# Four of eighteen key tiles transposed on TensorE instead of by DMA, in a two-branch attention layer

## The chip, the cores and the metric

The kernel runs on one core of one Trainium2 chip. The metric is the device time of one execution in microseconds (us); of several runs of the same kernel the median counts. [...]

## What is computed

One layer over 2048 latent tokens of width 1024, with 256 context tokens in front of the keys, so that each query sees 2304 keys. Two kinds of attention read the same projection: eight heads of latent attention (the first kind, `kind` 0: query and key of 96 columns, values of 64) and four heads of differential attention (the second kind, `kind` 1: two score maps of 64 columns each, values of 128). Both outputs pass gates and projections, are merged, projected again and normalised.

```python
def _softmax_attend(q, k, v, scale):
    s = jnp.einsum('bhqd,bhkd->bhqk', q, k).astype(jnp.float32) * scale
    p = jax.nn.softmax(s, axis=-1).astype(v.dtype)
    return jnp.einsum('bhqk,bhkd->bhqd', p, v)

def _diff_attend(q1, q2, k1, k2, v, lam, scale):
    s1 = jnp.einsum('bhqd,bhkd->bhqk', q1, k1).astype(jnp.float32) * scale
    s2 = jnp.einsum('bhqd,bhkd->bhqk', q2, k2).astype(jnp.float32) * scale
    p = jax.nn.softmax(s1, axis=-1) - lam * jax.nn.softmax(s2, axis=-1)
    return jnp.einsum('bhqk,bhkd->bhqd', p.astype(v.dtype), v)
...
    o_a = _blockwise(lambda q: _softmax_attend(q, k_mla, v_mla, MLA_SCALE), (q_mla,))
    o_d = _blockwise(lambda q1, q2: _diff_attend(q1, q2, k1, k2, dv, lam, DIFF_SCALE),
                     (dq[:, :, 0], dq[:, :, 1]))
```

## The kernel before

The kernel has three stages. The first (to about 930 us) projects the tokens and writes queries, keys, values and gates to DRAM. The second (about 935 to 2630 us) is the attention; the gate projections that the first stage left over fill its TensorE order as `gate_units` (tiles `fhT`, `fw`, `pf`, `fo`). The third merges, projects and normalises. Numbers are carried as a high part and a low part, so a product is two or three matmuls.

The attention runs over units of one head and 256 queries: 64 units of the first kind and 32 of the second, interleaved two to one (`units`, lines 810 to 814). A unit has two tiles of 128 queries. For such a tile `softmax_tile` computes the scores against the 2304 keys in three stretches of 768 columns, each in a PSUM tile `ps` of 1024 columns (pool `cps`, three buffers): per operand pair one matmul of 512 columns and one of 256 (line 669), three pairs for the first kind, two for each map of the second. VectorE empties `ps` into `s` and carries the running minimum along (line 670); ScalarE then makes the exponential of all 2304 columns in place (line 683) with the row sum. There are 256 such score tiles, 128 of each kind; in the second kind two maps are combined on VectorE (line 773) before they go on, which leaves 64.

`transposed` (line 689) then brings the 192 probability tiles into the layout that the product with the values needs, keys on the partitions. It takes a tile in two halves of 1152 columns, that is nine key tiles of 128: ScalarE casts the half to float16 (`hl`, line 693), GpSimd subtracts that from `s` for the low part (line 694; VectorE does one of two in the last units), and a DMA transpose on the SP queue (line 695) moves both parts as 18 blocks of 128x128 into `pts`. `hl` has four buffers, `pts` two units' worth, `s` five. Four units later in the written order the products with the values read `pts` through `pt_part` (lines 710, 723, 728).

`load_v` (line 790) makes the float16 parts of a head's values at the head's first unit, chunk by chunk of 384 columns: ScalarE scales and casts (line 804), VectorE scales again and subtracts (line 805). There are 48 chunks: three for each of eight heads, six for each of four.

The written order gives priorities; the final order on each engine is laid out ahead of the run by a planner that works with its own estimates of times. At run time each engine takes its instructions in that fixed order.

Of the kernel before, what the change touches and what calls it, by code (L numbers as in the profile page):

```python
# [9 lines left out]
F32 = mybir.dt.float32  # L10
F32R = mybir.dt.float32r
F16 = mybir.dt.float16
I32 = mybir.dt.int32
AF = mybir.ActivationFunctionType
ALU = mybir.AluOpType
PSUM = bass.MemoryType.PSUM
DRAM = bass.MemoryType.DRAM

P = 128
# [31 lines left out]
LEAD = 1  # L51
SPN = 3
LAG = 4

O_CQ, O_CKV, O_KR, O_GA, O_DQ, O_DK, O_DV, O_GD, O_MG = (
    0, 384, 640, 672, 1184, 1696, 2208, 2720, 3232)
# [5 lines left out]
def layer_kernel(ctx: ExitStack, tc: tile.TileContext, x, c, ctxt, c_ctx, w_mod, b_mod, w_in,  # L62
# [3 lines left out]
    pe, dve, act, pool, sp = nc.tensor, nc.vector, nc.scalar, nc.gpsimd, nc.sync  # L66
# [92 lines left out]
    with ExitStack() as st:  # L159
# [133 lines left out]
        for t in range(2):  # L293
            c0 = O_CKV + t * P
# [282 lines left out]

    with ExitStack() as st:
        kp, qp_, vp = {}, {}, {}
        kp[1] = st.enter_context(tc.tile_pool(name="ck1", bufs=3))  # L580
        qp_[1] = st.enter_context(tc.tile_pool(name="cq1", bufs=1))
        vr = st.enter_context(tc.tile_pool(name="cvr", bufs=2))
        vp[1] = st.enter_context(tc.tile_pool(name="cv1", bufs=1))
        kp[0] = st.enter_context(tc.tile_pool(name="ck0", bufs=3))
        qp_[0] = st.enter_context(tc.tile_pool(name="cq0", bufs=2))
        spool = st.enter_context(tc.tile_pool(name="cs", bufs=5))
        sm = st.enter_context(tc.tile_pool(name="csm", bufs=12))
# [5 lines left out]
        fr = st.enter_context(tc.tile_pool(name="fr", bufs=FB, side="right"))  # L593
        fw = st.enter_context(tc.tile_pool(name="fw", bufs=FB, side="right"))
        fo = st.enter_context(tc.tile_pool(name="fo", bufs=1, side="right"))
        ps_s = st.enter_context(tc.tile_pool(name="cps", bufs=3, space=PSUM))
        ps_f = st.enter_context(tc.tile_pool(name="cpf", bufs=1, space=PSUM))
        ps_o = st.enter_context(tc.tile_pool(name="cpo", bufs=1, space=PSUM))

# [61 lines left out]
        def softmax_tile(qk, ks, scale, shift, zsum):  # L661
            s = spool.tile([P, NT], F32, tag="s", name="s")
            z = sm.tile([P, 4], F32, tag="z", name="z")
            for g in range(3):
                ps = ps_s.tile([P, 1024], F32, tag="ps", name="ps")
                for i, (qa, sel) in enumerate(qk):
                    ka = sel(ks[g])
                    for c0, n in ((0, 512), (512, 256)):
                        pe.matmul(ps[:, c0:c0 + n], qa, ka[:, c0:c0 + n], start=(i == 0), stop=(i == len(qk) - 1))  # L669
                dve.tensor_scalar(s[:, g * 768:(g + 1) * 768], ps[:, :768], -scale, 3e38 if g == 0 else z[:, g - 1:g],  # L670
                                  op0=ALU.mult, op1=ALU.min, accum_out=z[:, g:g + 1])

            b = z[:, 2:3]
            if isinstance(shift, float):
                dve.tensor_scalar(z[:, 0:1], z[:, 2:3], z[:, 2:3], 2.0 ** 40, op0=ALU.mult, op1=ALU.is_lt)
                dve.tensor_scalar(z[:, 1:2], z[:, 0:1], shift, z[:, 2:3], op0=ALU.mult, op1=ALU.add)  # L676
                b = z[:, 1:2]
            elif shift is not None:
                dve.tensor_scalar(z[:, 0:1], z[:, 2:3], -1.0, z[:, 2:3], op0=ALU.mult, op1=ALU.min)
                dve.tensor_scalar(z[:, 0:1], z[:, 0:1], 2.0 ** -22, shift, op0=ALU.mult, op1=ALU.add)  # L680
                dve.tensor_scalar(z[:, 1:2], z[:, 0:1], z[:, 2:3], None, op0=ALU.add)
                b = z[:, 1:2]
            mark[0] = act.activation(s, s, AF.Exp, bias=b, scale=-1.0, accum_out=zsum).ins  # L683
            return s

        def new_pts():
            return [ptp.tile([P, 2, 9, 2, P], F16, tag="pt", name="pt") for _ in range(2)]

        def transposed(pts, i, s, shared):
            for e in range(2):  # L690
                hl = p16.tile([P, 2, 1152], F16, tag="hl", name="hl")
                se = s[:, e * 1152:(e + 1) * 1152]
                act.copy(hl[:, 0], se)  # L693
                (dve if shared and e else pool).tensor_tensor(hl[:, 1], se, hl[:, 0], op=ALU.subtract)  # L694
                sp.dma_start_transpose(pts[e][:, :, :, i, :].rearrange("p l k q -> p (l k) q"),
                                       hl.rearrange("p l n -> p (l n)"))

        def pt_part(pts, kt, l):
            return pts[kt // 9][:, l, kt % 9].rearrange("p i q -> p (i q)")

        def av_end(po, dst):
            o = op_.tile([P, 256], F32, tag="o", name="o")
# [46 lines left out]
        def mla_soft(h, u, qt, ks, pts):  # L749
            for i in range(2):  # L750
                qs = qt[0:96, :, i * P:(i + 1) * P]
                k_hi, k_lo = (lambda k: k[0:96, 0, :]), (lambda k: k[0:96, 1, :])
                s = softmax_tile([(qs[:, 0, :], k_hi), (qs[:, 0, :], k_lo), (qs[:, 1, :], k_hi)], ks, MLA_SCALE, LN_PSC,
                                 zs[u][:, i, h:h + 1])
                transposed(pts, i, s, n_ >= len(units) - 2)
                yield

        def diff_soft(h, u, qt, ks, pts):
            for i in range(2):
                def scores(m, shift, zsum):  # L760
                    qs = qt[:, m, :, i * P:(i + 1) * P]
                    km = (lambda k: k[:, m, :])
                    return softmax_tile([(qs[:, 0, :], km), (qs[:, 1, :], km)], ks, DIFF_SCALE, shift, zsum)


                za = zs[u][:, i, H + h:H + h + 1]
                sa = scores(0, lamc[:, 2:3], za)
                yield
                w = sm.tile([P, 3], F32, tag="w", name="w")
                sb = scores(1, None, w[:, 0:1])  # L770
                dve.reciprocal(w[:, 1:2], w[:, 0:1])
                dve.tensor_scalar(w[:, 2:3], za, w[:, 1:2], lamc[:, 0:1], op0=ALU.mult, op1=ALU.mult)
                dve.scalar_tensor_tensor(sa, sb, w[:, 2:3], sa, op0=ALU.mult, op1=ALU.add)  # L773
                transposed(pts, i, sa, n_ >= len(units) - 3)
                yield

        def load_k(kind, h):
            ks = []
            for g in range(3):
                k = kp[kind].tile([P, 2, 768], F32R, tag=f"k{kind}", name=f"k{kind}")  # L780
                cs = slice(g * 768, (g + 1) * 768)
                if kind == 0:
                    ldma(k[0:64], kn_s[h // 2][(h % 2) * 64:(h % 2) * 64 + 64, :, cs])
                    ldma(k[64:96], kr_s[:, :, cs])
                else:
                    ldma(k, dk_s[h][:, :, :, cs].rearrange("l d m n -> (l d) m n"))
                ks.append(k)
            return ks

        def load_v(kind, h):  # L790
# [10 lines left out]
            for t in range(0, NKT, nt):  # L801
                raw = vr.tile([P, nt, 64 * (1 + kind)], F32, tag="vr", name="vraw")
                ldma(raw, src[:, t:t + nt, :])
                act.activation(hi[:, t:t + nt, :], raw, AF.Identity, scale=sv)
                dve.scalar_tensor_tensor(lo[:, t:t + nt, :], raw, sv, hi[:, t:t + nt, :], op0=ALU.mult, op1=ALU.subtract)
            return vt


# [252 lines left out]
```

## Time and profile before

| | us |
|---|---|
| median of three runs | 3048.63 |
| lowest and highest run | 3046.4, 3067.55 |
| the profiled execution | 3054.12 |
| its span, first to last instruction | 3052.3 |
| TensorE busy | 2753.9 |
| VectorE busy | 1787.6 |
| GpSimd busy | 1581.8 |
| ScalarE busy | 1446.9 |

The profile is of one execution. A slice is a fortieth of the span, about 76 us. Idle time of an engine is put down to what ended it; matmuls overlap, so that the busy time of TensorE is not a measure of how fully it is used. PE is TensorE's matmuls, PEld its weight loads, DVE VectorE, ACT ScalarE, POOL GpSimd, SP the queue that issues most of the DMAs; a q behind an engine's name is its sequencer.

### The profile page before, as it was taken

Reading aid. Unit: us, or ns where it says so; the run is one execution under the profiler, and the core shown is the slowest. Engines: PE = TensorE matmul, PEld = TensorE weight load, DVE = VectorE, ACT = ScalarE, POOL = GpSimd, SP = SyncE. Lnnn points to the kernel's source line nnn. Section 1 sums busy time; section 2 is a strip of 40 time slices with the busy share of each in tenths; the row PEclk is TensorE's granted clock in tenths of the full one; section 3 lists DMA queues with packets and bytes.
Section 4 is the critical chain, followed back from the end, with each engine's and each line's share of the span. In section 5 each row is a group of like instructions: output and inputs, shape, how many; then the busy total and the mean of one; then the engine's idle time right before and its main releaser. Section 6 shows DMA issues by size and latency. Waiting matters only on the chain.

```text
span 3052.3 us, 44693 instructions
## 1 busy us (share of the span) xinstructions
PE 2753.9 (90%) x16177; PEld 2241.3 (73%) x16177; DVE 1787.6 (59%) x3583; ACT 1446.9 (47%) x1757; POOL 1581.8 (52%) x922
## 2 busy tenths in 40 slices
PE   7999999999998988979888899889889787789998
PEld 5888888879777766757666677667667665789886
DVE  4476310024766757767666577666676688575444
ACT  3333222233335656756666576656577566321110
POOL 2442222232444666857666567657567566363344
PEclk9999999999999999989999899989899898899999
DMA  8567533364487999999999999999999998977542
GB/s 253 128 184 226 158 90 97 94 217 140 133 245 193 206 195 200 194 220 214 188 207 198 236 226 205 204 189 182 222 209 205 196 209 164 241 210 210 181 137 89
DMA packets 1273377, 571.93 MB, mean 187 GB/s; under 512 B 950250, under 2 KB 1222336, under 8 KB 1273156
## 3 DMA queue, kind: packets, MB, share of 16 engines
q1 hardware_dynamic: 1149448, 463.59, 70.5%
q10 hardware_dynamic: 123708, 105.49, 15.0%
q8 instruction: 127, 2.08, 0.3%
q14 instruction: 94, 0.77, 0.1%
HBM read 224.16 MB, written 118.30 MB: 112 GB/s over the span
## 4 chain that ended last, share of the span: by engine, by line
DMA 20%; PE 18%; issue 6%; ACT 6%; DVE 6%; POOL 5%; ACTq 1%; SPq 1%; POOLq 0%; DVEq 0%
DMA pt<-hl 16%; PE pz L995 6%; PE ps L669 5%; POOL hl L694 4%; ACT s L683 3%; ACT hl L693 2%; DVE s L670 2%; PE po L723 1%; PE po L710 1%; DMA mg<-gt 1%; POOL fw L108 1%; PE po L728 1%; DMA fraw<-in_w_in_dram 1%; DMA g<-gt 1%; PE py L114 1%
## 5 line engine op out<-in xcount | busy, mean ns | idle before, releaser
L694 POOL TENSOR_TENSOR hl<-s,hl 128x1152 f16<-128x1152 f32 x378 | 939.9, 2502 | 470.7 <-ACT hl L693 432.7
L669 PE MATMUL ps<-k,q 96*128 96x256 f32 (+3 forms) x3840 | 840.1, 359 | 54.4 <-DVE s L670 47.2
L669 PEld LDWEIGHTS ps<-k,q 96*128 96x128 f32 (+1 forms) x3840 | 624.0, 197 | 176.3 <-DVE s L670 58.3
L670 DVE TENSOR_SCALAR_CACHE_REDUCE s<-ps,z 128x768 f32<-128x768 f32 x512 | 518.4, 1014 | 207.5 <-PE ps L669 197.7
L693 ACT CAST hl<-s 128x1152 f16<-128x1152 f32 x384 | 433.3, 1148 | 430.1 <-DMA pt<-hl 259.8
L683 ACT ACTIVATE s<-s,z 128x2304 f32<-128x2304 f32 x256 | 566.9, 2215 | 71.9 <-DVE z L676 34.2
L112 PE MATMUL pp<-hT,w 128*128 128x512 f32 (+1 forms) x896 | 350.3, 393 | 4.8 <-DVE qa L331 2.5
L108 POOL TENSOR_TENSOR w<-raw,w 128x512 fp32r<-128x512 f32 (+1 forms) x126 | 164.5, 1311 | 362.8 <-ACT w L105 346.3
L113 PE MATMUL pp<-hT,w 128*128 128x512 f32 (+1 forms) x896 | 351.8, 393 | 0.0
L114 PE MATMUL pp<-hT,w 128*128 128x512 f32 (+1 forms) x896 | 350.3, 392 | 0.0
L670 DVE TENSOR_SCALAR_CACHE_REDUCE s<-ps 128x768 f32<-128x768 f32 x256 | 243.9, 953 | 77.5 <-PE ps L669 66.7
L710 PE MATMUL po<-pt,vd 128*128 128x256 f16 x1728 | 237.3, 282 | 27.2 <-DMA pt<-hl 27.2
L723 PE MATMUL po<-pt,va 128*128 128x256 f16 x1152 | 177.3, 296 | 88.2 <-DMA pt<-hl 88.1
L710 PEld LDWEIGHTS <-vd 128*128 128x128 f16 x1728 | 157.9, 101 | 81.2 <-issue 50.5
L723 PEld LDWEIGHTS <-va 128*128 128x128 f16 x1152 | 107.3, 105 | 142.9 <-issue 91.5
L108 POOL TENSOR_TENSOR fw<-fraw,fw 128x512 fp32r<-128x512 f32 x84 | 143.3, 1706 | 120.2 <-ACT fw L105 114.4
L112 PEld LDWEIGHTS pp<-hT,w 128*128 128x128 f32 x896 | 170.1, 190 | 44.3 <-DVE qa L331 3.0
L114 PEld LDWEIGHTS pp<-hT,w 128*128 128x128 f32 x896 | 170.3, 190 | 38.2
L113 PEld LDWEIGHTS pp<-hT,w 128*128 128x128 f32 x896 | 170.3, 190 | 37.7 <-POOL hT L266 0.4
L773 DVE SCALAR_TENSOR_TENSOR s<-s,w 128x2304 f32<-128x2304 f32 x64 | 195.7, 3058 | 0.5
L995 PE MATMUL pz<-wz,yt 128*128 128x512 f32 x768 | 179.6, 396 | 0.8 <-DVE z L998 0.8
L995 PEld LDWEIGHTS pz<-wz,yt 128*128 128x128 f32 x768 | 144.3, 188 | 35.8 <-DVE z L998 1.3
(222 smaller groups left out, 4384.1 us busy)
## 6 DMA issues: line engine op xcount, KB each, us to landing
raw<-in_w_in_dram SPq DMA_DIRECT2D x122, 256.0 KB, 3.1
fraw<-in_w_in_dram ACTq DMA_DIRECT2D x79, 256.0 KB, 4.7
xt<-in_x_dram SPq DMA_DIRECT2D x32, 512.0 KB, 5.1
mg<-gt SPq DMA_DIRECT2D x64, 256.0 KB, 3.8
q<-dq ACTq DMA_DIRECT2D x60, 256.0 KB, 6.3
gt<-o SPq DMA_DIRECT2D x54, 256.0 KB, 2.0
gt<-fo ACTq DMA_DIRECT2D x42, 256.0 KB, 4.2
kn<-kst SPq DMA_DIRECT2D x36, 256.0 KB, 3.3
```

The costliest lines, as they stand in the source:

```text
L108: eng_lo.tensor_tensor(lo, t32, hi.bitcast(F32) if hi.dtype == F32R else hi, op=ALU.subtract)
L112: pe.matmul(ps, wh, mh, start=first, stop=False)
L113: pe.matmul(ps, wh, ml, start=False, stop=False)
L114: pe.matmul(ps, wl, mh, start=False, stop=last)
L669: pe.matmul(ps[:, c0:c0 + n], qa, ka[:, c0:c0 + n], start=(i == 0), stop=(i == len(qk) - 1))
L670: dve.tensor_scalar(s[:, g * 768:(g + 1) * 768], ps[:, :768], -scale, 3e38 if g == 0 else z[:, g - 1:g], op0=ALU.mult, op1=ALU.min, accum_ ...
L683: mark[0] = act.activation(s, s, AF.Exp, bias=b, scale=-1.0, accum_out=zsum).ins
L693: act.copy(hl[:, 0], se)
L694: (dve if shared and e else pool).tensor_tensor(hl[:, 1], se, hl[:, 0], op=ALU.subtract)
L710: pe.matmul(po, vv[:, w, kt, :], pt_part(pts, kt, l), start=(kt == 0 and i == 0), stop=(kt == NKT - 1 and i == 2))
L723: pe.matmul(po, vv[:, kt, :], pt_part(pts, kt, 0), start=(kt == 0), stop=(kt == NKT - 1))
L995: pe.matmul(pz[:, n, :], y[:, yy, k, :], wz[k][ww][:, n * 512:(n + 1) * 512], start=(k == 0 and i == 0), stop=(k == KT - 1 and i == 2))
```

## The change

In the first kind, four of the eighteen key tiles of each probability tile (tiles 5 to 8, the end of the first half) no longer go through the cast, the subtraction and the DMA transpose. TensorE transposes them in float32 into a PSUM tile `px` of 512 columns, ScalarE copies this as the high part into `pts`, and VectorE subtracts for the low part. The first DMA transpose of such a tile then has 10 blocks instead of 18; the second kind and the second half stay at 18. In `hl` and `pts` the high and low block of a key tile now lie side by side.

The scores are computed in stretches of 1024, 768 and 512 columns, each with a PSUM pool and a key tile of its own size. Per operand pair that is five matmuls instead of six. The space for `px` comes from this.

In `load_v`, GpSimd scales the loaded values in place, ScalarE casts them, and GpSimd subtracts.

```diff
+NCB = 5
+GS = ((0, 1024), (1024, 768), (1792, 512))
...
-        ps_s = st.enter_context(tc.tile_pool(name="cps", bufs=3, space=PSUM))
+        ps_s = [st.enter_context(tc.tile_pool(name=f"cps{g}", bufs=1, space=PSUM)) for g in range(3)]
+        ps_x = st.enter_context(tc.tile_pool(name="cpx", bufs=1, space=PSUM))
...
-            for g in range(3):
-                ps = ps_s.tile([P, 1024], F32, tag="ps", name="ps")
+            for g, (k0, nk) in enumerate(GS):
+                ps = ps_s[g].tile([P, nk], F32, tag="ps", name="ps")
                 for i, (qa, sel) in enumerate(qk):
                     ka = sel(ks[g])
-                    for c0, n in ((0, 512), (512, 256)):
-                        pe.matmul(ps[:, c0:c0 + n], qa, ka[:, c0:c0 + n], start=(i == 0), stop=(i == len(qk) - 1))
-                dve.tensor_scalar(s[:, g * 768:(g + 1) * 768], ps[:, :768], -scale, 3e38 if g == 0 else z[:, g - 1:g],
+                    for c0 in range(0, nk, 512):
+                        c1 = min(c0 + 512, nk)
+                        pe.matmul(ps[:, c0:c1], qa, ka[:, c0:c1], start=(i == 0), stop=(i == len(qk) - 1))
+                dve.tensor_scalar(s[:, k0:k0 + nk], ps, -scale, 3e38 if g == 0 else z[:, g - 1:g],
                                   op0=ALU.mult, op1=ALU.min, accum_out=z[:, g:g + 1])
...
-            return [ptp.tile([P, 2, 9, 2, P], F16, tag="pt", name="pt") for _ in range(2)]
+            return [ptp.tile([P, 9, 2, 2, P], F16, tag="pt", name="pt") for _ in range(2)]
-        def transposed(pts, i, s, shared):
-            for e in range(2):
-                hl = p16.tile([P, 2, 1152], F16, tag="hl", name="hl")
-                se = s[:, e * 1152:(e + 1) * 1152]
-                act.copy(hl[:, 0], se)
-                (dve if shared and e else pool).tensor_tensor(hl[:, 1], se, hl[:, 0], op=ALU.subtract)
-                sp.dma_start_transpose(pts[e][:, :, :, i, :].rearrange("p l k q -> p (l k) q"),
-                                       hl.rearrange("p l n -> p (l n)"))
+        def transposed(pts, i, s, shared, ncb):
+            for e, n in enumerate((ncb, 9)):
+                hl = p16.tile([P, 9, 2, P], F16, tag="hl", name="hl")[:, :n]
+                se = s[:, e * 1152:e * 1152 + n * P].rearrange("p (k q) -> p k q", q=P)
+                act.copy(hl[:, :, 0], se)
+                (dve if shared and e else pool).tensor_tensor(hl[:, :, 1], se, hl[:, :, 0], op=ALU.subtract)
+                sp.dma_start_transpose(pts[e][:, :n, :, i, :].rearrange("p k l q -> p (k l) q"),
+                                       hl.rearrange("p k l q -> p (k l q)"))
+            for k0 in range(ncb, 9, 4):
+                px = ps_x.tile([P, 4, P], F32, tag="px", name="px")
+                for t in range(4):
+                    pe.transpose(px[:, t, :], s[:, (k0 + t) * P:(k0 + t + 1) * P], ident)
+                hi, lo = (pts[0][:, k0:k0 + 4, l, i, :] for l in range(2))
+                act.copy(hi, px)
+                dve.tensor_tensor(lo, px, hi, op=ALU.subtract)
...
-                transposed(pts, i, s, n_ >= len(units) - 2)
+                transposed(pts, i, s, n_ >= len(units) - 2, NCB)
...
-                transposed(pts, i, sa, n_ >= len(units) - 3)
+                transposed(pts, i, sa, n_ >= len(units) - 3, 9)
...
-            for g in range(3):
-                k = kp[kind].tile([P, 2, 768], F32R, tag=f"k{kind}", name=f"k{kind}")
-                cs = slice(g * 768, (g + 1) * 768)
+            for g, (k0, nk) in enumerate(GS):
+                k = kp[kind].tile([P, 2, nk], F32R, tag=f"k{kind}{g}", name=f"k{kind}{g}")
+                cs = slice(k0, k0 + nk)
...
-                act.activation(hi[:, t:t + nt, :], raw, AF.Identity, scale=sv)
-                dve.scalar_tensor_tensor(lo[:, t:t + nt, :], raw, sv, hi[:, t:t + nt, :], op0=ALU.mult, op1=ALU.subtract)
+                pool.tensor_scalar(raw, raw, sv, None, op0=ALU.mult)
+                act.copy(hi[:, t:t + nt, :], raw)
+                pool.tensor_tensor(lo[:, t:t + nt, :], raw, hi[:, t:t + nt, :], op=ALU.subtract)
```

## Rows read from the trace of the kernel before

**Rows 1.** The page: engine busy us (share) xinstructions, then tenths in 40 slices.

```profile
PE 2753.9 (90%) x16177; PEld 2241.3 (73%) x16177; DVE 1787.6 (59%) x3583; ACT 1446.9 (47%) x1757; POOL 1581.8 (52%) x922
...
PEclk9999999999999999989999899989899898899999
DMA  8567533364487999999999999999999998977542
```

**Rows 2.** Stretches view, inner attention: us, busy by engine, clock, DMA share, GB/s.

```profile
1000.00:2500.00 1500.00, 1316.19 (x8035) 1024.98 (x8033) 1025.26 (x2099) 980.17 (x968) 979.85 (x423) 0.92 1.12 205
```

**Rows 3.** DMA view, 1000 to 2500 us: packets, MB, share; issues, median us to landing.

```profile
q1 hardware_dynamic: 806782, 206.83, 82.3%
q10 hardware_dynamic: 115168, 99.78, 29.0%
...
pt<-hl SPq DMA_TRANSPOSE x345, 6.8
```

**Rows 4.** Line 695 (ns min/median/max, first and last start), and SP's timeline from 1500 us.

```profile
L695 SPq DMA_TRANSPOSE pt<-hl x384: 2169/3342/14507, 961.4 to 2621.3; - x192
...
1497.88 142.65 SPq L695 DMA_TRANSPOSE pt<-hl  x34
```

**Rows 5.** The chain of work, 1000 to 2500 us: shares by line.

```profile
by line: DMA pt<-hl 32.0%; issue 10.7%; PE ps L669 9.6%; POOL hl L694 6.8%; ACT s L683 6.3%; ACT hl L693 3.9%; PE po L723 2.7%; DVE s L670 2.5%; POOL fw L108 2.1%; PE po L710 1.9%; PE po L728 1.9%; DMA fraw<-in_w_in_dram 1.8%; DVE s L773 1.
```

**Rows 6.** Waits from 950 to 2600 us: us in total, times, longest us.

```profile
PE po L723 <- DMA pt<-hl: 85.2, 25, 10.6
PE ps L669 <- DVE s L670: 47.2, 35, 4.7
PE po L710 <- DMA pt<-hl: 27.2, 17, 4.9
...
ACT hl L693 <- DMA pt<-hl: 258.0, 124, 12.8
```

**Rows 7.** TensorE's timeline, first stage: start us, us, engine, line, operation.

```profile
644.52 0.39 PE L112 MATMUL pp<-hT,w 128*128 128x512 f32 x1
644.75 1.03 PE L261 MATMUL pt<-ident,xt 128*128 128x128 f32 x8
645.54 0.48 PE L113 MATMUL pp<-hT,w 128*128 128x512 f32 x1
```

**Rows 8.** TensorE's timeline in the attention.

```profile
1321.92 4.39 PE L669 MATMUL ps<-k,q 96*128 96x512 f32 x24
1326.15 0.40 PE L114 MATMUL pf<-fhT,fw 128*128 128x512 f32 x1
1326.39 0.39 PE L112 MATMUL pf<-fhT,fw 128*128 128x512 f32 x1
```

**Rows 9.** Groups by line: shape xcount | busy us, mean ns | idle before, releasers.

```profile
L694 POOL TENSOR_TENSOR hl<-s,hl 128x1152 f16<-128x1152 f32 x378 | 939.9, 2502 | 470.7 <-ACT hl L693 432.7 <-DVE s L670 7.0 <-DVE z L680 6.6
...
L693 ACT CAST hl<-s 128x1152 f16<-128x1152 f32 x384 | 433.3, 1148 | 430.1 <-DMA pt<-hl 259.8 <-DVE s L773 68.0 <-PE ps L669 20.4
...
L805 DVE SCALAR_TENSOR_TENSOR va<-vraw,vsc,va 128x384 f16<-128x384 f32 x24 | 37.5, 1575 | 29.0 <-ACT va L804 29.0
...
L805 DVE SCALAR_TENSOR_TENSOR vd<-vraw,vsc,vd 128x384 f16<-128x384 f32 x24 | 29.7, 1254 | 9.9 <-ACT vd L804 9.9
```

**Rows 10.** Single lines: engine, operation, ns min/median/max, first and last start us.

```profile
L641 ACT ACTIVATE fo<-pf x42: 571/587/600, 955.1 to 2403.0; 128x512 f32<-128x512 f32 x42
...
L643 DVE SCALAR_TENSOR_TENSOR fo<-fo,pf x16: 671/682/689, 956.2 to 1941.0; 128x512 f32<-128x512 f32 x16
...
L926 POOL TENSOR_TENSOR uf<-ab x32: 720/742/1247, 2503.8 to 2824.2; 128x256 f32<-128x256 f32 x32
...
L872 POOL TENSOR_TENSOR rawe<-rawe,gb x16: 1270/1364/1891, 2661.7 to 2731.4; 128x512 f32<-128x512 f32 x16
```

**Rows 11.** Stretches of 50 us, columns as in rows 2.

```profile
1300.00:1350.00 50.00, 36.80 (x221) 28.71 (x220) 26.80 (x60) 26.55 (x26) 22.62 (x11) 0.86 1.17 225
...
1800.00:1850.00 50.00, 47.27 (x312) 36.40 (x311) 41.67 (x82) 36.74 (x38) 33.32 (x14) 1.00 1.17 220
```

More of the change, by code (lines that the diff above doesn't have):

```diff
@@ L579, in layer_kernel @@
         kp, qp_, vp = {}, {}, {}
-        kp[1] = st.enter_context(tc.tile_pool(name="ck1", bufs=3))
+        kp[1] = st.enter_context(tc.tile_pool(name="ck1", bufs=1))
         qp_[1] = st.enter_context(tc.tile_pool(name="cq1", bufs=1))
@@ L583, in layer_kernel @@
         vp[1] = st.enter_context(tc.tile_pool(name="cv1", bufs=1))
-        kp[0] = st.enter_context(tc.tile_pool(name="ck0", bufs=3))
+        kp[0] = st.enter_context(tc.tile_pool(name="ck0", bufs=1))
         qp_[0] = st.enter_context(tc.tile_pool(name="cq0", bufs=2))
@@ L686, in new_pts @@
         def new_pts():
-            return [ptp.tile([P, 2, 9, 2, P], F16, tag="pt", name="pt") for _ in range(2)]
-        def transposed(pts, i, s, shared):
-            for e in range(2):
-                hl = p16.tile([P, 2, 1152], F16, tag="hl", name="hl")
-                se = s[:, e * 1152:(e + 1) * 1152]
-                act.copy(hl[:, 0], se)
-                (dve if shared and e else pool).tensor_tensor(hl[:, 1], se, hl[:, 0], op=ALU.subtract)
-                sp.dma_start_transpose(pts[e][:, :, :, i, :].rearrange("p l k q -> p (l k) q"),
-                                       hl.rearrange("p l n -> p (l n)"))
+            return [ptp.tile([P, 9, 2, 2, P], F16, tag="pt", name="pt") for _ in range(2)]
[14 more added lines that the diff above has]
+                dve.tensor_tensor(lo, px, hi, op=ALU.subtract)
         def pt_part(pts, kt, l):
-            return pts[kt // 9][:, l, kt % 9].rearrange("p i q -> p (i q)")
+            return pts[kt // 9][:, kt % 9, l].rearrange("p i q -> p (i q)")
         def av_end(po, dst):
```

## The prediction

> **What bounds the kernel now.** I read the page first: TensorE is busy 90% of the span, and the slices show that the DMA engines run at 9 tenths or more through the middle half, just where TensorE's granted clock is no longer steady [rows 1]. That half is the attention stage, so everything below is read from it, mostly from its inner 1500 us. There TensorE is busy 1316 us, ScalarE 980, GpSimd 980, VectorE 1025, and the DMA share is 1.12, that is, packets of two queues overlap on the same engines all the time; the mean granted clock is 0.92 [rows 2]. [...]
>
> So no compute engine but TensorE is near its limit, and TensorE still idles 184 us. The DMA view of the same stretch says what fills the engines: 82.3% is the SP queue, 29.0% the ScalarE queue [rows 3]; in this stretch the SP queue is almost only the transposes of the split probabilities, 345 of them. The SP rows give the pace: 384 transposes between 961 and 2624 us, 4.3 us each, of which the issuing instruction alone holds the queue 3.34 us at the median, 2.17 at best, 14.5 at worst; the timeline shows 34 of them in one unbroken piece of 142.65 us, 4.2 us each [rows 4]. They run one behind another with little between them. The chain inside the stretch agrees: the landing of a transpose (`pt<-hl`) is 32.0% of it, four times any other single line but `issue` [rows 5]. The waits show how it reaches the engines: ScalarE stands 258 us in 124 waits because a `hl` buffer is not back from its transpose; GpSimd's idle time before the subtraction ends mostly with ScalarE's cast, 433 of 471 us [rows 9]; TensorE waits 85 and 27 us for `pt` and 47 us for VectorE to empty a score buffer [rows 6].
>
> The stage is thus paced by a loop, cast, subtract, transpose, buffer back, with TensorE close behind as the second limit.
>
> **The change part by part.** *Fewer transposed blocks.* A transpose moves 18 blocks of 128 columns (9 high, 9 low). For the first kind (128 score tiles of the 192 that are transposed) the first of two moves only 10. That is 128 of 384 transposes cut by 8/18, 14.8% of all blocks. The trace has no transpose of 10 blocks, so its price lies between no saving and the proportional one: 4.3 us x 8/18 x 128 = 245 us of queue time at the pace of [rows 4], 123 us at the best case of 2.17 us. The DMA share speaks for proportional: the engines are full of these packets, and their number falls with the blocks. What reaches the end is the part on the chain: 32.0% of the 1663 us stage is 532 us, and 14.8% of that is **79 us** saved. [...]
>
> *Shorter casts and subtractions.* The 1152-column subtraction on GpSimd takes 2.50 us, the cast on ScalarE 1.15 [rows 9]. With 640 columns I take the subtraction as proportional, -1.1 us x 128 = -136 us of GpSimd work. For ScalarE I use the line between 0.587 us at 512 columns (`fo`, [rows 10]) and 1.148 at 1152, about 0.70 at 640: -0.45 x 128 = -57 us of work. On the chain these lines are 6.8% and 3.9% [rows 5], 113 and 65 us of the stage; 15% of the first and 13% of the second are **17 and 8 us** saved. That the new layout of `hl` (high and low of a block side by side) is written in pieces of 128 costs nothing by any row here; if it slows GpSimd by a tenth, that is some 90 us of its work with 9% of the chain, 8 us.
>
> *The four blocks on TensorE.* 512 transposes of 128x128 in f32. The nearest rows are the transposes of x in the first stage: eight of them between two matmuls start at 644.75 and the next matmul at 645.54, 0.10 us each [rows 7]. That is 51 us of TensorE. [...] I take half: **+26 us**. They are emptied by ScalarE (128 x 0.587 = 75 us) and VectorE (128 x 0.682 = 87 us, the 512-column operation that reads PSUM) [rows 10]. ScalarE thus ends at +18 us, VectorE at +20 after losing the value split below. The ScalarE lines are 10.2% of the chain, so its added 75 us is taken at **+8 us**, VectorE's at +1.
>
> *New waits.* Before, TensorE never waited for the exponential; with five `s` buffers it could run several tiles ahead. Now its in-order queue has, once per tile of the first kind, a transpose that needs the exponential, and the next scores, the values' products and the gate projections stand behind it. ScalarE in turn waits for TensorE before it copies `px`, with the next exponential behind that copy. Bounds: nothing, if the order leaves room, and 128 x 2.1 us (the mean of ScalarE's 124 waits) = 269 us. The nearest wait of the same sort, TensorE for VectorE at a score buffer, is 47 us over 768 stretches; I take **+10 us**.
>
> *Stretches of 1024, 768, 512.* Columns are the same; one of six matmuls per operand pair goes. 24 score matmuls, 12 pairs of 512+256, take 4.23 us up to the next matmul's start, 0.352 a pair, and a lone 512-column matmul 0.24 to the next [rows 8], so the 256-column one costs about 0.12: half of a 512-column one, and two small ones cost what a large one does. No gain beyond the last eviction before the exponential, 512 instead of 768 columns; the first is longer by as much. Zero; with the buffers still three, a loss needs TensorE to wait for the 1024-column one, and the 47 us could grow by a third, 16 us.
>
> *Values on GpSimd.* 48 chunks of 384 columns lose a VectorE operation (37.5 and 29.7 us in all, [rows 9]) and gain two on GpSimd, a scaling and a subtraction. GpSimd takes 0.742 us for 256 columns and 1.364 for 512 [rows 10], so about 1.05 for 384: +101 us of work, in bursts of 6 us for a head of the first kind and 13 for the second, ahead of `hl` subtractions, which wait. At GpSimd's 9% of the chain it is **+9 us**; bounds 0 and 101.
>
> *The clock.* In [rows 11], 50 us stretches with 36.8 us of TensorE work have a granted clock of 0.86, those with 47.3 have 1.00: less waiting for `pt` gives clock back. [...]
>
> **Sum.** -79 -17 -8 +26 +8 +1 +10 +9 -10 = -60 us. The profiled execution took 3054.1 us (span 3052.3), so 2994 for its like; it lies 5.5 us above the median of the runs, so the forecast is **2989 us**, 2.0% faster. Its own range is 2950 to 3015.
>
> **The rivals.**
>
> *The queue frees the whole stage.* If transposes alone pace it, the queue's own saving counts, 123 to 245 us, less TensorE's 51. Speaking for it: the unbroken SP pieces and a DMA share over 1. Against: TensorE is busy 88% of the stretch and takes over soon. A saving of 110 to 170 us, about 2905.
>
> *TensorE is the bound, or the burden only moves.* The saved landing time is latency that the two units of buffered `pt` hide anyway, and TensorE's 51 us, GpSimd's 101 us burst and the new waits eat the rest. It also covers a short transpose that costs nearly what a long one does. Then the sum is -25 to +30 us, about 3045; with all 101 us of the value split on the path and the forecast's other terms it is +32, about 3080, the end of this case. [...]
>
> *Slower: TensorE stands at the transposes.* ScalarE is late by 2.1 us at 124 places now, and every one of these delays the exponential behind it; TensorE did not feel it, and now does. Price: with 1.2 us a tile on average, 128 x 1.2 = 154 us instead of my 10, the sum is +84 us, about 3130. It decides from 0.6 us a tile (77 us) on, where the sum is above zero. For it speaks that both in-order queues now wait for each other; against, that exponential and transpose can be placed some microseconds apart with other matmuls between them.
>
> **How the numbers follow.** Chances: forecast 0.44, whole stage freed 0.17, burden moves 0.23, TensorE stands 0.16. About 1% (30 us) is what a measurement of this kernel can tell from no change. Faster by over 1% takes the first two, 0.61; within 1% 0.23; slower 0.16. The range goes from 2900, the end of the second case, to 3070, the upper part of the third; it leaves out most of the fourth and a little of the second, some 0.2.
>
> **What would show it.** Right: the SP queue's transposes keep to 384 but a third of them at 10/18 of the time; DMA share in the stage near 1.0; ScalarE's wait for `pt<-hl` well under 258 us; the granted clock above 0.92. `px` waits of TensorE (on `s` from line 683's exponential) under 20 us in all. Wrong: that wait at 80 us or more (TensorE stands), a short transpose at 3 us (no saving), or GpSimd's `hl` late behind the value split.

## The result

| | before | after |
|---|---|---|
| median of the runs, us | 3047.52 (4 runs, 3034.46 to 3067.55) | 2967.98 (4 runs, 2960.77 to 2979.64) |
| the profiled execution, us | 3054.12 | 2964.99 |

The ratio is 0.9716, with a 95% interval from 0.9674 to 0.9758: 2.8% faster, where 2.0% was forecast (2989 us, range 2900 to 3070). In the two profiled executions the difference is 89 us where the sum said 60.

The page of the kernel after (engine busy us and share; in 40 slices the clock that TensorE was granted, in tenths of its full one, and DMA), to be held against [rows 1]:

```profile
PE 2761.3 (93%) x16049; PEld 2210.5 (75%) x16049; DVE 1777.4 (60%) x3663; ACT 1446.5 (49%) x1885; POOL 1522.9 (51%) x1018
...
PEclk9999999999999999999999999999999998899999
DMA  8467533364568999999999999999999998877542
```

TensorE does about the same busy time in a shorter span, and the slices of its clock that fell to 8 in the attention stage are gone until the very end of the stage. The inner 1500 us (columns as in [rows 2]) and the DMA view of the same stretch (as in [rows 3]):

```profile
1000.00:2500.00 1500.00, 1384.61 (x8279) 1044.20 (x8279) 1091.28 (x2309) 1026.16 (x1136) 956.20 (x520) 0.96 1.04 193
```

```profile
q1 hardware_dynamic: 727232, 187.35, 75.1%
q10 hardware_dynamic: 116446, 100.94, 28.7%
...
pt<-hl SPq DMA_TRANSPOSE x362, 5.7
```

TensorE's idle time in these 1500 us went from 184 to 115 us, its clock from 0.92 to 0.96, the DMA share from 1.12 to 1.04, and 362 transposes fit where 345 did, with a tenth fewer packets. The waits from 950 to 2600 us, as in [rows 6]:

```profile
PE po L737 <- DMA pt<-hl: 34.2, 9, 6.6
PE ps L674 <- DVE s L675: 21.2, 20, 3.4
PE po L724 <- DMA pt<-hl: 20.9, 15, 4.8
PE px L707 <- DVE pt L710: 20.0, 8, 8.7
...
PE px L707 <- ACT s L688: 2.3, 2, 1.9
...
ACT hl L700 <- DMA pt<-hl: 197.2, 82, 10.8
...
ACT pt L709 <- PE px L707: 19.7, 12, 4.4
```

TensorE's two waits for `pt` fell from 112 to 55 us, its wait for score buffers from 47 to 21. The new wait on the exponential is 2.3 us in all; the new wait that does show is 20.0 us for the one `px` tile to be emptied.

The single prices stand in the groups by line and shape (columns as in [rows 9]):

```profile
L701 POOL TENSOR_TENSOR hl<-s,hl 128x640 f16<-128x640 f32 x128 | 181.2, 1415 | 100.0 <-ACT hl L700 94.2 <-DVE z L686 2.8 <-DVE pt L710 1.0
...
L700 ACT CAST hl<-s 128x640 f16<-128x640 f32 x128 | 92.3, 721 | 79.2 <-DMA pt<-hl 65.6 <-DMA k<-kn 8.0 <-POOL hl L701 2.3
L710 DVE TENSOR_TENSOR pt<-px,pt 128x512 f16<-128x512 f32 x128 | 87.8, 686 | 147.4 <-ACT pt L709 146.9 <-DMA q<-qn 0.3
L707 PE MATMUL px<-ident,s 128*128 128x128 f32 x512 | 81.9, 285 | 22.4 <-DVE pt L710 20.0 <-ACT s L688 2.3
...
L709 ACT CAST pt<-px 128x512 f16<-128x512 f32 x128 | 73.5, 574 | 28.1 <-PE px L707 19.7 <-issue 4.6 <-POOL fw L110 1.8
```

All of them are near what was put down: 1.42 us for the short subtraction (1.39 by proportion), 0.72 for the short cast (0.70), 0.574 and 0.686 for emptying `px` (0.587 and 0.682).

### The profile page after: what moved, and what is told of

Read it like the earlier page. It is cut to its first block, busy times and chain, and to the rows that moved or that the text cites. A ratio compares the mean times of both kernels' runs of the same rounds, so it can differ in the third digit from the quotient of the medians.

```text
span 2963.2 us, 44826 instructions
## 1 busy us (share of the span) xinstructions
PE 2761.3 (93%) x16049; PEld 2210.5 (75%) x16049; DVE 1777.4 (60%) x3663; ACT 1446.5 (49%) x1885; POOL 1522.9 (51%) x1018
## 5 line engine op out<-in xcount | busy, mean ns | idle before, releaser
L701 POOL TENSOR_TENSOR hl<-s,hl 128x1152 f16<-128x1152 f32 (+1 forms) x378 | 784.6, 2092 | 440.6 <-ACT hl L700 408.7
L674 PE MATMUL ps<-k,q 96*128 96x512 f32 (+3 forms) x3200 | 822.3, 391 | 25.0 <-DVE s L675 21.8
L674 PEld LDWEIGHTS ps<-k,q 96*128 96x128 f32 (+1 forms) x3200 | 546.1, 193 | 145.2 <-DVE s L675 38.4
L700 ACT CAST hl<-s 128x1152 f16<-128x1152 f32 (+1 forms) x384 | 375.5, 1007 | 362.0 <-DMA pt<-hl 197.2
L675 DVE TENSOR_SCALAR_CACHE_REDUCE s<-ps,z 128x768 f32<-128x768 f32 (+1 forms) x512 | 450.4, 880 | 104.8 <-PE ps L674 84.3
L675 DVE TENSOR_SCALAR_CACHE_REDUCE s<-ps 128x1024 f32<-128x1024 f32 x256 | 312.1, 1219 | 129.7 <-PE ps L674 106.2
L787 DVE SCALAR_TENSOR_TENSOR s<-s,w 128x2304 f32<-128x2304 f32 x64 | 183.5, 2867 | 0.1
L710 DVE TENSOR_TENSOR pt<-px,pt 128x512 f16<-128x512 f32 x128 | 87.8, 686 | 147.4 <-ACT pt L709 146.9
```

Source lines behind the costliest of these rows:

```text
L674: pe.matmul(ps[:, c0:c1], qa, ka[:, c0:c1], start=(i == 0), stop=(i == len(qk) - 1))
L675: dve.tensor_scalar(s[:, k0:k0 + nk], ps, -scale, 3e38 if g == 0 else z[:, g - 1:g], op0=ALU.mult, op1=ALU.min, accum_out=z[:, g:g + 1])
L700: act.copy(hl[:, :, 0], se)
L701: (dve if shared and e else pool).tensor_tensor(hl[:, :, 1], se, hl[:, :, 0], op=ALU.subtract)
```

## The experiments

Each ratio is to the kernel before, measured beside it on the same chip (its median there 3053 to 3060 us). Moving one part lets the planner lay out a new order for every engine. In the traces, ScalarE, VectorE and GpSimd run the attention stage of e9 in exactly the changed kernel's order, instruction by instruction; in e2, e5, e10 and e12 they do not, and neither do e1, e3 and e4 keep the order of the kernel before. So each of these runs tests its part together with a new order.

| run | median us | ratio, 95% interval |
|---|---|---|
| e1: no blocks on TensorE | 3091.94 | 1.0096 (1.0061 to 1.0131) |
| e2: values back on VectorE | 2973.28 | 0.9730 (0.9684 to 0.9777) |
| e3: stretches alone | 3069.26 | 1.0046 (1.0021 to 1.0071) |
| e4: value split alone | 3055.98 | 0.9986 (0.9959 to 1.0013) |
| e5: all blocks moved anyway | 3061.74 | 1.0008 (0.9967 to 1.0050) |
| e6: TensorE's blocks as an extra | 3094.84 | 1.0145 (1.0099 to 1.0190) |
| e7: eight blocks | 3085.91 | 1.0122 (1.0080 to 1.0163) |
| e8: both kinds | 2977.03 | 0.9763 (0.9724 to 0.9802) |
| e9: old layout | 2966.44 | 0.9695 (0.9652 to 0.9738) |
| e10: a buffer of its own | 3050.72 | 0.9984 (0.9954 to 1.0014) |
| e11: eight blocks, `px` in halves | 3591.41 | 1.1761 (1.1699 to 1.1824) |
| e12: five shared buffers | 2972.97 | 0.9731 (0.9692 to 0.9770) |

The theory was that fewer transposed blocks make the gain and that TensorE is the next limit. The rivals were that the stretches, the relief of VectorE, or the shorter casts and subtractions make it.

### Which part carries the gain: e1 to e4

e1 is the changed kernel with all 18 key tiles on the DMA:

```diff
-NCB = 5
+NCB = 9
...
-        ps_x = st.enter_context(tc.tile_pool(name="cpx", bufs=1, space=PSUM))
+        ps_x = None
```

> The changed kernel with all 18 key tiles back on the DMA transpose; the stretches, the layout of hl and pt and the values on GpSimd stay. If fewer transposed blocks are the cause (theory), nearly the whole gain of 80 us goes: 3030 to 3065 us, with 384 transposes at 4.2 us or more apart and a DMA share of 1.1 in the stage. If the stretches, the layout or the value split carry the gain (rivals), it stays under 3000 us.

It took 3092 us, 1.0% slower than the kernel before and above the expected range. Not only the gain goes, what is left of the change costs something. Its inner stage and its transposes (ns min/median/max):

```profile
1000.00:2500.00 1500.00, 1287.86 (x7302) 960.14 (x7300) 960.83 (x2020) 957.07 (x950) 1031.70 (x494) 0.92 1.11 201
```

```profile
L702 SPq DMA_TRANSPOSE pt<-hl x384: 2380/3322/14449, 946.4 to 2629.8; - x192
```

Clock, DMA share and transposes are those of [rows 2, 4].

e2 takes the changed kernel and puts `load_v` back as it was:

```diff
-                pool.tensor_scalar(raw, raw, sv, None, op0=ALU.mult)
-                act.copy(hi[:, t:t + nt, :], raw)
-                pool.tensor_tensor(lo[:, t:t + nt, :], raw, hi[:, t:t + nt, :], op=ALU.subtract)
+                act.activation(hi[:, t:t + nt, :], raw, AF.Identity, scale=sv)
+                dve.scalar_tensor_tensor(lo[:, t:t + nt, :], raw, sv, hi[:, t:t + nt, :], op0=ALU.mult, op1=ALU.subtract)
```

> The changed kernel with the value split back on VectorE. Theory: worth little either way, 2950 to 2985 us; the sum of the prediction had it at +9 us, so about 2960 without it. If the relief of VectorE carries the gain (rival), 3000 us or more.

2973 us: no difference to the changed kernel that the intervals show.

e3 is the kernel before with the stretches of 1024, 768 and 512 columns and the key tiles that go with them:

```diff
+GS = ((0, 1024), (1024, 768), (1792, 512))
...
-            for g in range(3):
-                ps = ps_s.tile([P, 1024], F32, tag="ps", name="ps")
+            for g, (k0, nk) in enumerate(GS):
+                ps = ps_s[g].tile([P, nk], F32, tag="ps", name="ps")
```

> The kernel before with scores in stretches of 1024, 768 and 512 columns and nothing else. Theory: 3030 to 3065 us, as before, since the columns are the same and a 256-column matmul costs half of a 512-column one. If the sixth matmul or the shorter last eviction counts (rival), 3000 us or less, with less waiting of TensorE for the score buffers than 47 us.

3069 us, 0.5% slower and 4 us above the expected range: the sixth matmul showed no gain, and the stretches are a small price, about 14 us, for the PSUM space that `px` needs. TensorE's wait for score buffers did fall, to 34.4 us, while its waits for `pt` at the three lines of the value products rose from 124 us in all (88, 27 and 9, from 950 to 2650 us) to 180 (92, 49 and 39). Why is not settled; the order is new too.

e4 is the kernel before with the value split of the change (the diff of e2 the other way round):

> The kernel before with the value split on GpSimd and nothing else. Theory: 3040 to 3075 us, no change that counts. If its 101 us of GpSimd work hold back the subtractions and so the transposes, up to 3130 us; if the relief of VectorE carries the gain (rival), 3000 us or less.

3056 us, no change. So neither the stretches nor the relief of VectorE carries the gain: it goes when the four key tiles return to the cast, the subtraction and the DMA transpose.

### Blocks moved, or shorter casts: e5 and e6

e5 leaves the whole change in place and adds one transpose of 8 blocks from the same `hl` into a tile that nobody reads, so 18 blocks move as before:

```diff
                 sp.dma_start_transpose(pts[e][:, :n, :, i, :].rearrange("p k l q -> p (k l) q"),
                                        hl.rearrange("p k l q -> p (k l q)"))
+                if n < 9:
+                    xd = xtp.tile([P, 8, P], F16, tag="xd", name="xd")
+                    sp.dma_start_transpose(xd, hl[:, :4].rearrange("p k l q -> p (k l q)"))
```

> The changed kernel, but after each transpose of 10 blocks the SP queue transposes 8 blocks of the same hl tile into a tile that nobody reads: 18 blocks as before, while casts, subtractions and TensorE's blocks stay as changed. If the moved blocks are the cause (theory), the time goes back to 3040 to 3100 us. If the shorter casts and subtractions carry the gain (rival), it stays at 2970 to 3000 us. In the prediction's sum the two had 79 and 25 us, which would be about 3045.

3062 us: the gain is gone, 0.9716 became 1.0008, some 89 us. Inner stage, and the SP queue's instructions on `hl` (ns min/median/max):

```profile
1000.00:2500.00 1500.00, 1334.21 (x7840) 1002.20 (x7839) 1029.08 (x2175) 973.04 (x1074) 931.12 (x499) 0.94 1.13 203
```

```profile
L703 SPq DMA_TRANSPOSE pt<-hl x384: 1319/2951/13557, 951.7 to 2611.7; - x192
...
L707 SPq DMA_TRANSPOSE xd<-hl x128: 1231/1434/7127, 971.5 to 2610.4; - x128
```

The DMA share is back at 1.13. A transpose of 8 blocks takes 1.43 us at the median, 8/18 of the 3.34 of [rows 4] would be 1.49: at this size the price is near the proportional one, which was the open bound of the prediction. This run gives back two things at once, the traffic and the time for which `hl` is held until its blocks have left; it does not tell them apart. It also has another order than the changed kernel (ScalarE's differs from the 39th instruction after 930 us on), so the 89 us are not the price of the blocks alone. That the queue is loaded again shows in how long a tile stood ready: from the end of its subtraction to the start of its transpose into `pt` it was 3.3 us on average before, 2.1 in the changed kernel and 3.9 in e5.

e6 is e1 with TensorE's four blocks done on top, into a tile that nobody reads, while all 18 key tiles still go by DMA:

```diff
-NCB = 5
+NCB = 9
+XCB = 5
...
-            for k0 in range(ncb, 9, 4):
+            for k0 in range(XCB, 9, 4) if i_first else ():
...
-                hi, lo = (pts[0][:, k0:k0 + 4, l, i, :] for l in range(2))
+                xd = xpp.tile([P, 4, 2, P], F16, tag="xd", name="xd")
+                hi, lo = (xd[:, :, l, :] for l in range(2))
```

> The kernel with all 18 key tiles on the DMA (3092 us) and TensorE's four blocks done on top of it into a tile that nobody reads: the price of TensorE's part with no relief. By the prediction's terms (26, 8, 1 and 10 us) about 3135 us; if TensorE's idle time takes it in while the transposes pace the stage, 3085 to 3105; if the wait for the exponential costs a microsecond per tile (the slower rival), 3200 or more.

3095 us, against 3092 of e1; by the ratios (each to its own runs of the kernel before) 0.5% or 15 us more, with overlapping intervals. TensorE's part is almost free while something else paces the stage. Its two waits there, 950 to 2650 us:

```profile
PE ps L676 <- DVE s L677: 34.7, 32, 6.4
PE px L709 <- DVE xd L713: 33.9, 13, 6.1
```

From e6 to e5 the casts and subtractions become shorter while the number of blocks moved stays: 1.0145 to 1.0008, about 42 us, give or take 19. The transposes take the SP queue the same time in both (1400 and 1412 us in all), so it is not the queue's own work that differs, but the order does. That both sources count, the moved blocks more, is therefore likely and not shown; the two runs do not split the gain cleanly.

How much an order alone can do is seen from the spread. All kernels that move 18 blocks per transpose, or 18 in two, with six different orders, lie at 3048 to 3095 us (before, e1, e3, e4, e5, e6). Of those with 10 blocks and one `px` hand-over per tile, five lie at 2966 to 2977 us in four orders (the changed kernel, e2, e8, e9, e12); the sixth, e10 below, does not.

### Is TensorE the next limit: e7, e8 and e11

e7 sets `NCB = 1`, so that eight key tiles of the first kind go through TensorE, in two rounds of `px`:

> The changed kernel with eight key tiles of the first kind through TensorE instead of four (NCB = 1; the first transpose moves 2 blocks). If the transposes still pace the stage, it gains again by what the first four did, 2870 to 2920 us. If TensorE is the limit now (theory: busy 92% of the inner stage at clock 0.96), its 51 us more are paid and little comes back: 2960 to 3010 us.

3086 us, outside both expectations, slower than the kernel before. The queue is relieved, as the stage shows, but the engines now wait for each other (950 to 2650 us):

```profile
1000.00:2500.00 1500.00, 1353.00 (x8040) 1035.35 (x8039) 1042.08 (x2187) 949.50 (x1147) 783.52 (x484) 0.95 0.83 160
```

```profile
PE px L707 <- DVE pt L710: 45.6, 29, 8.4
PE ps L674 <- DVE s L675: 37.1, 33, 6.7
PE po L737 <- ACT pt L709: 33.1, 20, 7.3
...
ACT hl L700 <- DMA pt<-hl: 188.2, 99, 13.7
ACT pt L709 <- PE px L707: 107.9, 46, 7.0
...
DVE pt L710 <- ACT pt L709: 152.9, 67, 12.9
...
DVE s L675 <- PE px L707: 52.0, 26, 3.9
```

The DMA share is down to 0.83, so neither the amount of transfers nor that of TensorE's work (1353 us busy, less than after's 1385) sets the pace. TensorE stands for VectorE to empty `px`, ScalarE for TensorE to fill it, and the scores' evictions stand behind. ScalarE's longest wait is still the one for `hl`: 188 us, hardly less than the changed kernel's 197, with fewer blocks to move. So the loop over `hl` is not out of it.

e11 asks whether the single `px` buffer is to blame: the same eight key tiles, with `px` used as two halves of two blocks in turn.

```diff
-NCB = 5
+NCB = 1
...
+        px_all = ps_x.tile([P, 2, 2, P], F32, tag="px", name="px")
...
-            for k0 in range(ncb, 9, 4):
-                px = ps_x.tile([P, 4, P], F32, tag="px", name="px")
-                for t in range(4):
+            for k0 in range(ncb, 9, 2):
+                px = px_all[:, (k0 - ncb) // 2 % 2]
+                for t in range(2):
```

> The kernel with eight key tiles through TensorE (3086 us), with px used as two halves of two blocks in turn, so that TensorE can fill one while the other is emptied; casts and subtractions from px double in number at half the size. If the single px buffer made that kernel slow, 2970 to 3020 us. If it is that TensorE, ScalarE and VectorE stand for each other in order (theory: 108 us ScalarE for px, 33 us TensorE for pt written by ScalarE, 52 us VectorE for px), 3060 us or more.

3591 us, 17.6% slower. Twice as many hand-overs TensorE to ScalarE to VectorE and back, with 128x256 emptyings, and the waits grow with them (950 to 2650 us):

```profile
PE po L738 <- ACT pt L710: 89.7, 73, 12.4
PE px L708 <- DVE pt L711: 76.7, 64, 4.0
...
ACT pt L710 <- PE px L708: 234.9, 138, 5.4
...
DVE pt L711 <- ACT pt L710: 418.8, 156, 16.7
```

The same columns in twice as many hand-overs cost some 500 us more than e7, so it is the hand-overs that cost, not the columns. But the run does not answer its question. TensorE never filled one half while the other was being emptied: in none of the 511 cases did the next pair of transposes start before VectorE had finished with the pair before. The halves share one PSUM tile, and in the trace they are used strictly one after the other. From the first transpose to the end of VectorE's subtraction a filling takes 2.8 us on average; 512 of them are 1440 us, 256 in e7 at 4.8 are 1230, 128 in the changed kernel at 6.0 are 770. Whether the single buffer made e7 slow stays open; two real buffers were not tried. What e7 and e11 show is kin to the prediction's slower rival, with the emptying of `px` in place of the exponential: with one hand-over per tile it stays small, with two the gain is gone.

e8 takes four key tiles through TensorE in the second kind as well (`transposed(pts, i, sa, n_ >= len(units) - 3, NCB)`):

> The changed kernel with four key tiles through TensorE in the second kind as well: 64 more tiles, 26 us more for TensorE, 7.4% fewer transposed blocks. If the transposes still pace the stage, 2920 to 2940 us; if TensorE is the limit now (theory), 2960 to 2995 us.

2977 us, with an interval that overlaps the changed kernel's: 512 blocks fewer, 7.4% of the 6912 of the kernel before, bring nothing more, net of 64 more hand-overs through `px`.

### Layout and buffers: e9, e10 and e12

e9 keeps all high blocks ahead of all low ones in `hl` and `pt`, as before, by views of flat tiles:

```diff
-                hl = p16.tile([P, 9, 2, P], F16, tag="hl", name="hl")[:, :n]
+                hl = p16.tile([P, 18 * P], F16, tag="hl", name="hl")[:, :2 * n * P]
```

> The changed kernel with the order of before in hl and pt: all high blocks, then all low ones. The runs so far leave some 20 us against the change (all 18 tiles on the DMA with stretches, layout and value split: 3092 us; stretches alone 3069, value split alone 3056). If the layout costs them, this gives 2945 to 2955 us. If they came with the planned order of that one kernel (theory, since the casts, subtractions and transposes take the same time each in both layouts: 1.15, 2.39 and 3.3 us), 2960 to 2980 us.

2966 us: the layout is worth nothing either way, and with the same order on the engines this is the cleanest of the comparisons. e1's 1.0096 is thus 1.0046 for the stretches and a remainder of some 19 us (give or take 16) that no single part shows; it may lie in the order that the planner made for that kernel, but that was not tested.

e10 gives the short `hl` one buffer of its own beside the four for 18 blocks:

```diff
-                hl = p16.tile([P, 9, 2, P], F16, tag="hl", name="hl")[:, :n]
+                hl = p16.tile([P, n, 2, P], F16, tag=f"hl{n}", name="hl", bufs=4 if n == 9 else 1)
```

> The changed kernel with a buffer of its own for the 10-block hl beside the four of 18 blocks. ScalarE still waits 197 us for hl buffers. If that loop still sets the pace, 2920 to 2950 us; if TensorE is the limit now (theory: 92% busy), 2955 to 2985 us.

3051 us, outside both expectations. One buffer more in all, the same blocks moved, and the whole gain is lost. The SP queue's share from 1000 to 2500 us, the waits from 950 to 2650 and the group of short casts:

```profile
q1 hardware_dynamic: 686027, 174.98, 72.9%
```

```profile
PE po L737 <- DMA pt<-hl: 78.6, 17, 11.8
PE po L724 <- DMA pt<-hl: 42.0, 11, 16.2
...
ACT hl L700 <- DMA pt<-hl: 195.3, 67, 18.9
```

```profile
L700 ACT CAST hl<-s 128x640 f16<-128x640 f32 x128 | 92.5, 723 | 169.4 <-DMA pt<-hl 151.9 <-PE po L742 5.1 <-POOL hl L701 4.3
```

ScalarE waits as long in total as in the changed kernel, but in fewer and longer pieces, and now mostly before the short casts: 152 us against 66 in the changed kernel. A short cast has to wait for its one buffer, and what comes after it in ScalarE's fixed order waits too. (The longest wait, 18.9 us, is that of a long cast.) TensorE's waits for `pt` are back at 121 us, where the kernel before has 115 in the same stretch. So the theory in its first form falls: fewer blocks moved are not enough for the gain. That `hl` buffers must also come back in time for the next cast fits these waits; how much of the loss is the one buffer itself and how much the order that the planner made around it stays open.

e12 is the counterpart: five buffers shared by both lengths, paid for with the second buffer of the loaded values.

```diff
-        vr = st.enter_context(tc.tile_pool(name="cvr", bufs=2))
+        vr = st.enter_context(tc.tile_pool(name="cvr", bufs=1))
...
-        p16 = st.enter_context(tc.tile_pool(name="c16", bufs=4))
+        p16 = st.enter_context(tc.tile_pool(name="c16", bufs=5))
```

> The changed kernel with five hl buffers that both lengths share instead of four; the space comes from the second buffer of the loaded values, which 12 head changes use. The run with a single buffer of its own for the short hl lost the whole gain (3051 us) though it moved as few blocks, so buffers count beside the blocks. If the return of hl buffers still sets the pace, 2920 to 2950 us, and ScalarE's 197 us of waiting for them falls by half. If TensorE is the limit of the changed kernel, 2955 to 2985 us; if one value buffer costs more than the fifth hl brings, 2985 to 3010 us.

2973 us, as the changed kernel, while ScalarE's wait for `hl` (950 to 2600 us) falls by a fifth, to 158 us, not by half:

```profile
1000.00:2500.00 1500.00, 1375.07 (x8271) 1039.81 (x8270) 1087.13 (x2314) 1031.85 (x1132) 958.93 (x520) 0.97 1.02 192
```

```profile
ACT hl L700 <- DMA pt<-hl: 157.8, 87, 7.8
```

In the changed kernel the loop of cast, subtraction, transpose and buffer seems no longer to set the pace: neither a fifth buffer (e12) nor fewer blocks (e8) gains. Both runs pay for what they give, e12 with a value buffer and e8 with TensorE's work and more hand-overs, so a small gain could be hidden. A tile stands ready for its transpose 4.7 us on average in e12 and 4.2 in e10, both with five buffers to stand in, one without loss and one with it: that time tells that the queue is loaded, not what it costs. That TensorE has taken over fits its 92% busy time in the inner stage; no run took work from TensorE alone, so this is argued and not shown. No version measured beats the changed kernel beyond its interval.

## Why the prediction was right, point by point

**What bounds the stage.** Right, as far as the runs go: in the kernels that move all blocks, e5 among them, there is no gain. One piece of evidence for it does not carry. The 34 transposes in one unbroken piece [rows 4] were taken to say that they run one behind another. The kernel after has the same picture, on SP's timeline and in the instructions of the line:

```profile
1497.73 145.70 SPq L702 DMA_TRANSPOSE pt<-hl  x33
```

```profile
L702 SPq DMA_TRANSPOSE pt<-hl x384: 1268/2842/12009, 954.9 to 2536.7; - x192
```

The timeline joins neighbours of one kind whatever lies between them; the durations have to be added up. Those 33 issuing instructions, added up, take 100 of the 146 us. The 34 before take 127 of 143, with four pauses of 1 to 5 us, so what the prediction read was nearly true, though not from that line. Over the whole stage it is 1424 of 1663 us before, 86%, and 1146 of 1584 after, 72%. Most of the rest ends when the next subtraction does, so no transpose was ready, and there buffers, the cast and the subtraction can count beside the blocks. A slip beside it: the chain's 32.0% for the landing is 3.3 times the next line's 9.6%, not four times.

**Fewer blocks, -79 us.** e5 puts it at about 89, with a new order in it. The proportional price was near enough: 1.43 us at the median for 8 blocks, and a best case of 1.27 for 10 against 2.17 for 18.

**Shorter casts and subtractions, -25 us.** The durations were right (1.42 and 0.72 us); the effect was perhaps larger, about 42 us from e6 to e5, give or take 19 and with a new order in it. A possible reason, argued and not shown: each cast and each subtraction is also time for which an `hl` buffer is not free, and the chain's shares of the two lines, 6.8% and 3.9%, do not hold that.

**Four blocks on TensorE, +26 +8 +1, and new waits, +10.** This is the term that was most wrong: 45 us put down, about 15 measured, give or take 17, so not clear of zero (e6 against e1, with a new order). That is its price in a kernel where the transposes set the pace; in the changed kernel, with TensorE busier, it was not measured. There too the work seems to have fallen into idle time: TensorE's busy share of the inner stage rose from 88 to 92% while the stage became shorter. The wait on the exponential is 2.3 us in all, as the prediction had it under 20; the wait that came instead was for VectorE to empty the one `px` tile, 20.0 us, which the prediction did not name.

**Stretches, 0.** Slightly wrong: 14 us slower (e3), near the bound of 16 that was given, though by more waiting for `pt` and not for score buffers, as that bound assumed.

**Values on GpSimd, +9.** The price of the work was right in sum, the effect was nil (e2, e4). The scaling and the two subtractions, ns min/median/max:

```profile
L818 POOL TENSOR_SCALAR vraw<-vraw,vsc x48: 1238/1247/3632, 879.3 to 2365.8; 128x384 f32<-128x384 f32 x48
...
L820 POOL TENSOR_TENSOR vd<-vraw,vd x24: 903/924/1382, 883.0 to 2173.9; 128x384 f16<-128x384 f32 x24
L820 POOL TENSOR_TENSOR va<-vraw,va x24: 912/922/3226, 936.4 to 2372.0; 128x384 f16<-128x384 f32 x24
```

That is 1.25 + 0.92 us per chunk, 104 us in all at the medians, where 101 were put down. That they meet a GpSimd with room at the 12 head changes is likely and was not tested. For the same chunk GpSimd's two instructions take 2.17 us where VectorE's one, which scales and subtracts at once, took 1.57 or 1.25 [rows 9]. In the `hl` subtraction, the same work on both engines, VectorE took 1.43 us on average and GpSimd 2.44 (1152 columns, kernel after, 6 and 250 of them); in the kernel before it was 2.07 and 2.50 (6 and 378).

**The clock, -10.** Right in direction, 0.92 to 0.96 in the inner stage. No run shows the 10 us, and none separates what the clock was worth. What the traces show in its place: the granted clock is either 1.00 or 0.50, and of the inner 1500 us it is 0.50 for 225 us before and for 116 us after. It goes with TensorE's idle time: in these 1500 us of the kernel before, TensorE stood idle for 3 us or more 17 times, and each time the clock fell to 0.50 between the start of the idle time and 2 us after its end.

**The rivals.** The whole stage freed was priced at 110 to 170 us; by its own figures, 123 to 245 less 51, it was 72 to 194, and the 89 us lie in that, so the total alone does not rule it out. The queue does: the transposes' time on it fell by 278 us (1424 to 1146) and the stage by 78. Something else set the pace for the difference. The burden did not merely move: TensorE's waits for `pt` halved. The slower rival did not happen at four blocks; at eight something like it did.

So the forecast was right in mechanism and sign, and a third too small. That it came so near is partly luck: by e1 to e6, TensorE's term cost some 30 us less, the casts and subtractions gave some 17 more, the blocks 10 more and the values cost nothing instead of 9, while the stretches and the open remainder of e1 took some 33 back. Errors of both signs cancelled. The differences for the blocks and for the casts lie within their intervals, and every one of these runs has a new order in it.

## What to carry to other kernels

Where a loop over a few buffers paces a stage, count what holds a buffer from its first write to its release: shortening a member of the loop may gain more than its own share of the chain (here about 42 us, give or take 19, where the shares gave 25). Work moved to an engine with idle time can be nearly free (e6: 15 us, give or take 17). Moving a part can win where moving twice as much loses (2968 and 3086 us): here each hand-over went through a single buffer between engines with a fixed order and stalled what was queued behind it (ScalarE's wait for `px` was 20 us in the kernel after and 108 in e7), so count the hand-overs, and read from the trace whether two halves of a buffer are really used at the same time (in e11 never, in 511 cases). A buffer reserved for one size did worse here than one fewer that all share (3051 and 2968 us). Where every change lets a planner lay out a new order, a run that gives one part back tests the order as well.

## What the runs showed of the hardware that was not expected

A DMA transpose's price on the queue goes down with its blocks, but not to nothing. At best it is 2.17 us for 18 blocks before, 1.27 for 10 after, 1.23 for 8 (e5), and in e7, where a third of the transposes have 2 blocks, the shortest takes 1.17:

```profile
L702 SPq DMA_TRANSPOSE pt<-hl x384: 1167/2756/11162, 948.1 to 2661.8; - x192
```

With transposes and subtractions paired in the order of time, which is roughly right, the median of those with 2 blocks in e7 is 1.2 us, of those with 10 in the kernel after 1.5, of those with 18 there 3.2. From 18 to 10 blocks the price about halves; from 10 to 2 it falls little. On GpSimd, scaling 128x384 in float32 in place by a column takes 1.25 us, longer than the two-input subtraction of the same size into float16 with 0.92. And 128x128 transposes in float32 between matmuls, 512 of them, left no loss clear of the noise as long as another part of the stage was slower (e6: 15 us, give or take 17).
